# Where a first norm's squares are made, and which bank holds a sixth row: a change to the opening stage of a two-layer recurrent decoder step

## The chip, the cores and the metric

The kernel runs on one core of one Trainium2 chip. The metric is the device time of one execution in microseconds (us), smaller being better. The time before the change is 1043.81 us, the median of 3 runs (1042.59 to 1045.02).

In the profile the engines are PE (TensorE, matrix products), DVE (VectorE), ACT (ScalarE), POOL (GpSimd) and SP (SyncE, which here issues most of the DMAs). Each engine works through its own instructions in the order in which the program lists them.

## The reference, cut to what matters

The reference is one step of a decoder with two layers: a gated linear recurrence with a short convolution (RG-LRU) and then a layer with a matrix state (HGRN2). There are 1024 prompt tokens and 32 sample tokens, 1056 columns in all. Everything is float32. The change touches the first lines of the first layer:

```python
def _rmsnorm(x, gain):
    y = x * lax.rsqrt(jnp.mean(x * x, axis=-1, keepdims=True) + EPS)
    return y * gain

def _lru_layer(x, g_norm, w_in, ...):
    xn = _rmsnorm(x, g_norm)
    u = xn @ w_in                       # 1024 -> 2 * 1536
    xb, gate = u[..., :W_LRU], u[..., W_LRU:]
    xc, new_buf = _causal_conv(xb, conv_w, conv_b, buf)
    h, h_last = _rg_lru(xc, w_r, b_r, w_i, b_i, lam, h0)
    y = h * silu(gate)
    return x + y @ w_out, h_last, new_buf
```

The scale `rsqrt(mean(x*x))` is one number for each token. It can be applied before the product or, because the product is linear, to its result.

## The kernel before, in words

**Tiles.** The activations lie transposed: 8 tiles (k = 0 to 7) of 128 features by 1056 tokens, cut into 3 chunks of 352 tokens. A float32 product is made from three faster matmuls: every operand is split into a high part (a cast, on ACT) and a low part (the difference, on DVE or POOL), and `mm3` (lines 288 to 290) adds high by high, high by low and low by high. One output row of 128 features for one chunk is 8 steps of k, so 24 matmuls, collected in one PSUM bank. There are eight banks: four of the tag `mm`, which take the rows in turn, and four of the tag `hg`, used in turn for norms and for the small products of the recurrence.

**The opening stage** (`start`, `begin`, `products`, lines 947 to 1018) makes six output rows (three gate rows, then three convolution rows) for each chunk.
- *Chunk 0* goes unnormed. Its x is multiplied by the gain and split as it lands (lines 958, 959), and its scale is applied when a row leaves its bank: line 610 for a gate row, line 563 for a convolution row. The scale comes from `squares` (line 481: the squares at line 488 on POOL or line 490 on ACT, their sum over k by the DVE additions of line 492) and from `norm` (line 496): a sum over features by PE (line 325), mean plus EPS by DVE (line 505), the power -0.5 by POOL (line 530), a diagonal by DVE (lines 531, 534), its spreading over 128 partitions by PE (line 536) and a copy to SBUF by ACT (line 990). That copy is what lines 610 and 563 multiply with.
- *Chunks 1 and 2* are normed ahead of their products. `token_norm` loads their tokens a second time, tokens by features (t0, t1, t2), squares and sums them on ACT (line 523), and spreads the scale in the same way (lines 524, 530, 531, 534, 536). `scaled_parts` then multiplies x by gain and scale (line 541, DVE), casts it (line 542, ACT) and subtracts (line 373, DVE, for two of eight tiles POOL).

Before the change four of the eight squares (k = 1, 3, 5, 7, the tuple `MU`) are made by POOL and four by ACT, through two buffers in turn. The weights of a row come in halves: `w0a`, `w0b` to `w5a`, `w5b`. Each half is loaded (line 358), cast on ACT (line 432) and subtracted (line 373), on DVE for rows 0, 1, 2 and 4 and on POOL for rows 3 and 5. Row 4 of chunk 0 has a `hg` bank (`ASIDE`); row 5 takes an `mm` bank again, the one that row 0 used.

**Order.** `Flow` (line 61) collects every operation with its engine, an estimated duration and its data dependences. `run` plans forward, then backward (`back`), which gives every operation its latest start as a key; smaller keys go first among the operations that are ready. It does so eight times, then tries 3000 random changes to the keys of the first 60 us (`search`), and issues all engines' instructions in the planned order. A second `Flow` does the same for the second layer, starting from the times at which the first leaves its buffers. Operations with a `chain` keep the order in which they were added: `FIRST_S` and `FIRST_Q` are the first loads on the ACT and SP queues, `FIRST` the order in which ACT and DVE prepare what has landed, `NEXT` the further loads on the SP queue. In them `x0` is a tile of chunk 0, `X0` one of chunk 1, `P` and `hc` small parameters.

Of the kernel before, what the change touches and what calls it, by code (L numbers as in the profile page):

```python
# [24 lines left out]
NW, NXO, NRAW = 4, 3, 3  # L25
# [8 lines left out]
SPOTS, SPOTS0, SPOTS1 = (-1, -1, 0, 2), (2, 5, -1, -1), (1, 5, 9, 13, 17, 20)  # L34
K2 = 8 - K1
MEAN = 4.0
ASIDE = (4,)
ASIDE_W = ()
FIRST_S = "x0 g0 w0b x4"
FIRST_Q = "w0a x1 x2 x3 x5 x6 x7 w1a w1b"  # L40
FIRST = "w0a x0 x1 x2 x3 w0b x4 x5 x6 x7 w1a w1b"
NEXT = "w2a w2b t0 w3a w3b t1 w4a w4b -w4a t2 X0 X1 X2 X3 w5a w5b X4 X5 X6 X7 P hc"
RM, SM = 3, 6
OUT = ((0, 512), (512, 288), (800, 256))

# [15 lines left out]
class Flow:  # L61
# [9 lines left out]
    def __init__(self, until=None, side=1.2, busy=None, given=None):  # L71


        self.until = until
        self.busy = {e: (busy or {}).get(e, 0.0) for e in self.ENGINES}
        self.exact = busy is not None
        self.side = side
        self.ops = []
        self.writer = {}
        self.readers = {}  # L80
        self.main = None
        self.chain = {}
        self.soft = set()
        self.given = given or {}
        self.born = []
        self.lead = {}

    def add(self, eng, us, emit, r=(), w=(), prio=5, kb=0, main=False, both=False, line=None):

# [140 lines left out]
    def run(self, tries=0, first=0.0):  # L230
        self.after = [[] for _ in self.ops]
        for i, o in enumerate(self.ops):
            for d in o[3]:
                self.after[d].append(i)
        best = got = self.plan([o[4] for o in self.ops])
        for _ in range(self.TURNS):
            got = self.plan(self.back(got[2], got[4]))
            self.ends.append(got[0])
            best = min(best, got, key=lambda g: g[0])
        if tries:  # L240
            best = self.search(best, tries, first)
        self.log = [(i, self.ops[i][0], best[1][i], best[2][i]) for i in best[3]]
        for i in best[3]:
            self.ops[i][2]()
# [12 lines left out]
def tile_trunk(ctx: ExitStack, tc: tile.TileContext, xT, xN, prm, hc, w0, wg, wo0, w1, wo1, s_in,  # L257
               yT, h_out, c_out, sp_out, ss_out):
    nc = tc.nc
    V, S, G, T, Q = nc.vector, nc.scalar, nc.gpsimd, nc.tensor, nc.sync  # L260
# [13 lines left out]
    P = const.tile([128, NPRM], F32, name="prm_sb")  # L274
# [8 lines left out]
    def chunk(c):  # L283
        return slice(c * CH, (c + 1) * CH)
# [34 lines left out]
    def spans(n):  # L319
        return [(a, min(128, n - a)) for a in range(0, n, 128)]  # L320
# [23 lines left out]
    with ExitStack() as l0:  # L344
        pl = l0.enter_context(tc.tile_pool(name="l0", bufs=1, reuse_waits="tile"))
        fl = Flow("PE")

        def fixed(name, shape, dt=F32, pool=None):
            return (pool or pl).tile(shape, dt, tag=name, name=name)

        def ring(name, n, cols=CH, dt=F32):
            return cycle([(pl.tile([128, cols], dt, tag=f"{name}{i}", name=f"{name}_{i}"), (name, i)) for i in range(n)])
# [8 lines left out]
        def act(n, emit, r, w, prio=5, more=0.0, chain=None):  # L361
            fl.add("ACT", (0.09 + 0.00088 * n if fl.exact else 0.25 + 0.0007 * n) + more, emit, r, w, prio, line=chain)
# [5 lines left out]
        def pool(n, emit, r, w, prio=5):  # L368
            fl.add("POOL", 0.13 + 0.0022 * n if fl.exact else 0.1 + 0.00245 * n, emit, r, w, prio)
# [16 lines left out]
        t0 = fixed("t0", [128, 3, NB])  # L386
# [4 lines left out]
        xbs = ring("xb", 3, 384)  # L391
        ks = [(KR[:, chunk(i)], ("k", i)) for i in range(KB)]
        ts, xrs = cycle(ks[:3]), cycle(ks[3:])
        xos = ring("xo", NXO)
# [88 lines left out]
        def squares(k, x, xk, acc, eng=None, own=None, mult=False, chains=(None, None)):  # L483

            a, ak = acc
            sq, sk = next(own or ts) if k else acc
            if mult:
                pool(CH, lambda: G.tensor_tensor(sq[:, :CH], x, x, op=ALU.mult), (xk,), (sk,), 2)
            else:
                act(CH, lambda: S.activation(sq[:, :CH], x, AF.Square), (xk,), (sk,), 2, chain=chains[0])  # L490
            if k and eng is V:
                dve(CH, lambda: V.tensor_tensor(a[:, :CH], a[:, :CH], sq, op=ALU.add), (sk, ak), (ak,), 2, chain=chains[1])
            elif k:
                pool(CH, lambda: G.tensor_tensor(a[:, :CH], a[:, :CH], sq, op=ALU.add), (sk, ak), (ak,), 2)
# [14 lines left out]
        def token(c, i, prio, chain=None):  # L509

            (t, tk), (a, u) = tspots[c][i], spans(CH)[i]
            q = slice(c * CH + a, c * CH + a + u)
            dma(t[:u, :D], xN[q], (), tk, prio, 4 * u, chain=chain)
# [415 lines left out]
        free = [(R2[s][:, i, j], ("R", s, i, j)) for s in range(2) for i in range(2) for j in range(3)]  # L929
        raw = (halves[1][:8], [slots[i] for i in (4, 7, 5, 8)] + [halves[1][8], free[8], free[0], free[1]], free[2:8] + free[9:11])  # L930
        g0s = [g0[:, k:k + 1] for k in range(KD)]
        sqs, bcs = cycle([next(xos) for _ in range(NXO - 1)]), next(xos)
        acc, MU = next(xbs), (1, 3, 5, 7)
        VI = (0, 1, 2, 4)
        tspots = ((), ((rows[0], [slots[i][1] for i in range(3)]), (KR[:, :D], [k for _, k in ks[:3]]),
                       (R[:, 3], [("R", 1, 1, j) for j in range(3)])),
# [10 lines left out]
        def start():  # L947

            steps = {"P": [lambda q, c: dma(P, prm, (), (("P",),), 0, 74, q, c)],
                     "g0": [lambda q, c: dma(g0, prm[:, PRM["g0"][0]:PRM["g0"][1]], (), (("g0",),), 0, 4, q, c)]}  # L950
            for k, (x, xk) in enumerate(raw[0]):
                a, b = xh[k][:, chunk(0)], xl[k][:, chunk(0)]

                def load(q, c, k=k, x=x, xk=xk):
                    dma(x, xT[k][:, chunk(0)], (), (xk,), 0, 180, q, c)

                def parts(chains, k=k, x=x, xk=xk, a=a, b=b):
                    act(CH, lambda: S.activation(a, x, AF.Copy, scale=g0s[k]), (xk, ("g0",)), (("xh", k, 0),), 1, chain=chains[0])
                    dve(CH, lambda: V.scalar_tensor_tensor(b, x, g0s[k], a.bitcast(F32), op0=ALU.mult, op1=ALU.subtract),
                        (xk, ("g0",), ("xh", k, 0)), (("xl", k, 0),), 1, True, chains[1])  # L960

                steps[f"x{k}"] = load, parts
            for i in range(6):
                ahead = []
                row(i, ahead)
                for j, (load, split) in zip("ab", ahead):
                    steps[f"w{i}{j}"] = lambda q, c, load=load: load(q=q, chain=c), split
            steps.update({f"t{i}": [lambda q, ch, i=i: token(1, i, 1.0, ch)] for i in range(3)})
            steps.update({f"X{k}": [lambda q, ch, k=k: fetch(1, (k,))] for k in range(KD)})
            steps["hc"] = [lambda q, ch: dma(hct, hc, (), (("hct",),), 2, 196, q, ch)]  # L970
            for q, names in ((S, FIRST_S), (Q, FIRST_Q)):
                for n in names.split():
                    steps[n][0](q, str(q))
            done = FIRST.split()
            for n in done:
                steps[n][1](("ACT0", "DVE0"), *([G] if n in ASIDE_W else []))
            for n in NEXT.split():
                if n[0] == "-":
                    steps[n[1:]][1]()
                    done.append(n[1:])  # L980
                else:
                    steps[n][0](Q, SPQ)
            for i in range(6):
                for j in "ab":
                    if f"w{i}{j}" not in done:
                        steps[f"w{i}{j}"][1]()
            for k, (x, xk) in enumerate(raw[0]):
                squares(k, x, xk, acc, V, sqs, k in MU, ("ACT0", "DVE0"))
            bc, bk = norm(acc, next(xrs))
            act(CH, lambda: S.copy(bcs[0], bc), (bk,), (bcs[1],), 0)  # L990

        def fetch(c, ks=range(KD)):

            for k in ks:
                x, xk = raw[c][k]
                dma(x, xT[k][:, chunk(c)], (), (xk,), (0, 1.4, 1.9)[c], chain=SPQ)
# [7 lines left out]
        def products(c):  # L1004
            for i in (2, 0, 1, 3, 4, 5) if c else range(6):
                items[i][1](c, *product(ws[i], xcols(c), 1, later[i], next(hg) if not c and i in ASIDE else None), *([] if c else [bcs]))

# [46 lines left out]
    with ExitStack() as l1:  # L1054
        p1 = l1.enter_context(tc.tile_pool(name="l1", bufs=1, reuse_waits="tile"))
        last = {e: max(t[3] for t in fl.log if t[1] == e) for e in Flow.ENGINES}
        fl = Flow(side=0.4, busy={e: max(0.0, t - last["PE"]) for e, t in last.items()}, given=fl.times(last["PE"]))
# [651 lines left out]
        for k in range(H):  # L1709
            if k < 4:  # L1710
                olds = [("x", 1, k, x) for x in range(2)] + [("T", 1, i, k, x) for i in range(2) for x in range(2)]
            else:
                n, i = ((2, 0), (3, 0), (4, 0), (4, 1))[k - 4]
# [36 lines left out]
        x2 = [Gs, R[:, 3], R[:, 2], R[:, 1], Bs, B2, VT, Gc]  # L1750
# [5 lines left out]
        for n, (m, c) in enumerate([(m, c) for c in range(NCH) for m in range(2)] + [(m, c) for m in range(2, KD) for c in range(NCH)]):  # L1756
# [9 lines left out]
            x, xk = x2[m][:, chunk(c)], ykeys(Y2 + m, c * CH, CH)  # L1766
# [13 lines left out]
        for m in range(KD):  # L1780
# [4 lines left out]
            raw, rk = next(raws)  # L1785
# [12 lines left out]
        accs, sqs, dgs, sb = cycle(spare[:2]), cycle(spare[2:5]), cycle(spare[5:7]), spare[7]  # L1798
# [47 lines left out]
        for a, n in OUT:  # L1846
# [3 lines left out]
            acc, ak = next(accs)  # L1850
            for m in range(KD):
# [13 lines left out]
                x, xk = x2[m][:, q], ykeys(Y2 + m, a, n)  # L1865
# [88 lines left out]
```

## Time and profile before

| | |
|---|---|
| median of 3 runs | 1043.81 us |
| the profiled execution's own time | 1044.79 us |
| its span, first to last instruction | 1043.0 us |
| mean granted TensorE clock | 0.995 |
| PE busy | 1030.1 us, 99% of the span |
| DVE, ACT, POOL busy | 793.5, 590.4, 502.1 us |

The span leaves 1.8 us of the execution's time outside. A timeline row gives the start, the duration, the engine, the line and operation, the tile written and the tiles read, and in brackets how long the engine sat idle before it and what ended that. "x2" is two instructions merged in one row. `PEclk` is the clock that the throttle granted, as a part of full speed. A row of the windows view gives for each engine the busy time in that stretch and, behind an x, the number of instructions that started there.

### The profile page before, as it was taken

The page shows a single profiled execution, that of the slowest core. Times are in us where ns is not written, and L with a number is a line of the kernel's source. Part 1 is how long each engine was busy: PE and PEld are TensorE (multiplying, and loading weights), DVE is VectorE, ACT ScalarE, POOL GpSimd, SP SyncE. Part 2 cuts the span into 40 slices and gives each one's busy share as a digit, 9 for nine tenths or more (in the row PEclk, how much of TensorE's full clock was granted, in tenths as well). Part 3 has the DMA queues.
Part 4 walks back from the last instruction along what each step waited for, and adds up shares of the span by engine and source line. Part 5 has one row for each costly group of instructions (what it writes and reads, how often), then busy time and mean ns, then how long its engine had stood idle before and what let it go on. Part 6 is the DMA issues. An engine that isn't in the chain of part 4 may idle for free.

```text
span 1043.0 us, 25410 instructions
## 1 busy us (share of the span) xinstructions
PE 1030.1 (99%) x9794; PEld 1001.2 (96%) x9794; DVE 793.5 (76%) x1539; ACT 590.4 (57%) x1345; POOL 502.1 (48%) x587
## 2 busy tenths in 40 slices
PE   9899999999999999999999999999999999999997
PEld 9899999999999999999999999999999999989986
DVE  6899997888897599345498987877969696984436
ACT  6678656877775775334445464647464555752324
POOL 3325343444534355643527565554645555641544
PEclk9999999999999999999999999999999999999998
DMA  9511112123661586544655151423233242666204
GB/s 295 182 29 50 51 53 75 55 63 98 212 200 52 160 275 182 155 135 154 215 162 154 59 170 45 149 72 123 86 106 122 87 139 85 220 189 210 87 1 167
DMA packets 92809, 133.55 MB, mean 128 GB/s; under 512 B 11728, under 2 KB 70096, under 8 KB 92688
## 3 DMA queue, kind: packets, MB, share of 16 engines
q1 hardware_dynamic: 82896, 115.50, 35.3%
q10 hardware_dynamic: 9792, 16.43, 4.9%
q8 instruction: 77, 1.26, 0.5%
q14 instruction: 44, 0.36, 0.1%
HBM read 88.81 MB, written 38.20 MB: 122 GB/s over the span
## 4 chain that ended last, share of the span: by engine, by line
PE 95%; DMA 2%; issue 1%; DVE 1%; POOL 0%; SPq 0%; ACTq 0%; ACT 0%; POOLq 0%; DVEq 0%
PE mm L288 27%; PE mm L290 26%; PE mm L289 26%; PE hg L1185 2%; PE hg L650 1%; PE hg L1399 1%; PE hg L288 1%; PE hg L1401 1%; PE hg L289 1%; PE hg L290 1%; PE hg L1347 1%; DMA k<-in_xN_dram 1%; PE mm L1347 1%; PE hg L1443 1%; DMA wraw<-in_w_dram 1%
## 5 line engine op out<-in xcount | busy, mean ns | idle before, releaser
L288 PE MATMUL mm<-xh,whi 128*128 128x352 f32 (+1 forms) x1127 | 351.4, 312 | 0.0
L290 PE MATMUL mm<-xh,wlo 128*128 128x352 f32 (+1 forms) x1127 | 347.7, 308 | 0.0
L289 PE MATMUL mm<-xl,whi 128*128 128x352 f32 (+1 forms) x1127 | 347.3, 308 | 0.0
L373 POOL TENSOR_TENSOR wlo<-wraw,whi 128x256 fp32r<-128x256 f32 (+3 forms) x180 | 193.8, 1095 | 199.8 <-ACT whi L432 102.3
L289 PEld LDWEIGHTS mm<-xl,whi 128*128 128x128 f32 x1127 | 212.3, 188 | 1.5
L288 PEld LDWEIGHTS mm<-xh,whi 128*128 128x128 f32 x1127 | 211.7, 188 | 1.7
L290 PEld LDWEIGHTS mm<-xh,wlo 128*128 128x128 f32 x1127 | 212.0, 188 | 0.0
L288 PE MATMUL mm<-t,whi 128*128 128x264 f32 (+1 forms) x330 | 96.8, 293 | 1.3 <-DVE sg L1641 1.3
L582 DVE SCALAR_TENSOR_TENSOR k<-xb,prm_sb,k 128x352 f32<-128x352 f32 (+2 forms) x144 | 87.8, 619 | 12.9 <-ACT k L579 9.3
L290 PE MATMUL mm<-t,wlo 128*128 128x264 f32 (+1 forms) x330 | 94.4, 286 | 0.0
L289 PE MATMUL mm<-t,whi 128*128 128x264 f32 (+1 forms) x330 | 94.3, 286 | 0.0
L373 POOL TENSOR_TENSOR wlo<-R,whi 128x256 fp32r<-128x256 f32 x78 | 67.2, 887 | 44.5 <-ACT whi L1564 32.6
L1641 DVE TENSOR_TENSOR k<-mm,k 128x264 f32<-128x264 f32 x118 | 49.7, 425 | 22.9 <-PE mm L290 22.3
L665 POOL TENSOR_TENSOR k<-X 128x352 f32<-128x352 f32 x36 | 42.9, 1200 | 48.8 <-DVE R L666 39.0
L288 PEld LDWEIGHTS mm<-t,whi 128*128 128x128 f32 x330 | 62.0, 188 | 2.6 <-DVE sg L1641 1.8
L290 PEld LDWEIGHTS mm<-t,wlo 128*128 128x128 f32 x330 | 62.1, 188 | 0.0
L289 PEld LDWEIGHTS mm<-t,whi 128*128 128x128 f32 x330 | 62.1, 188 | 0.0
L432 ACT CAST whi<-wraw 128x512 fp32r<-128x512 f32 (+2 forms) x79 | 43.9, 572 | 25.7 <-PE mm L289 9.7
L288 PE MATMUL mm<-yh,whi 128*128 128x352 f32 x153 | 50.0, 327 | 0.0
L289 PE MATMUL mm<-yl,whi 128*128 128x352 f32 x153 | 49.4, 323 | 0.0
L290 PE MATMUL mm<-yh,wlo 128*128 128x352 f32 x153 | 49.4, 323 | 0.0
L1564 ACT CAST whi<-R 128x512 fp32r<-128x512 f32 x39 | 24.1, 617 | 35.1 <-PE mm L289 33.2
(479 smaller groups left out, 2521.5 us busy)
## 6 DMA issues: line engine op xcount, KB each, us to landing
wraw<-in_w_dram SPq DMA_DIRECT2D x54, 256.0 KB, 3.2
wraw<-in_w_dram ACTq DMA_DIRECT2D x34, 256.0 KB, 3.5
wraw<-in_wo_dram SPq DMA_DIRECT2D x34, 192.0 KB, 2.5
R<-in_w_dram ACTq DMA_DIRECT2D x19, 256.0 KB, 2.8
si<-in_s_in_dram SPq DMA_DIRECT2D x8, 512.0 KB, 5.6
vt<-sg SPq DMA_DIRECT2D x8, 512.0 KB, 3.3
sg<-vt SPq DMA_DIRECT2D x32, 128.0 KB, 3.0
kt<-kt SPq DMA_DIRECT2D x8, 512.0 KB, 2.6
```

The lines of the kernel that those rows point to most:

```text
L288: T.matmul(out, wh, xh, start=first, stop=False, skip_group_check=more)
L289: T.matmul(out, wh, xl, start=False, stop=False, skip_group_check=more)
L290: T.matmul(out, wl, xh, start=False, stop=last, skip_group_check=more)
L373: emit = lambda: e.tensor_tensor(b, x, a.bitcast(F32), op=ALU.subtract)
L432: act(m, lambda: S.copy(hi[:, :m], raw[:, :m]), rk, (hk,), prio, chain=chains[0])
L582: dve(u, lambda src=src, dst=dst, sh=sh, k=k: V.scalar_tensor_tensor(dst, sh(src, k), pc("cw", 12 * k + m), dst, op0=ALU.mult, op1=ALU.add ...
L650: fl.add("PE", 0.62, lambda ps=ps, i=i, c=c: T.matmul(ps[:96, :CH], gs[:, i, :], ST[:96, chunk(c)], start=True, stop=True), (("gs",), *((" ...
L665: pool(CH, lambda x=x, a=a, b=b: G.tensor_tensor(x, a.bitcast(F32), b.bitcast(F32), op=ALU.add), (ak, bk), (xk,), 3)
L1185: T.matmul(ps[32 * j:32 * j + 32, n * w:n * w + w], B[:, o:o + 32], q(slice(o, o + 32)), start=True, stop=True, tile_position=(0, 32 * j))
L1347: T.matmul(ps[:, n * 128:(n + 1) * 128], kt[:, 4 * i + n, :], vt[:, 4 * i + n], start=True, stop=True)
L1564: act(512, lambda: S.copy(hi, raw), (rk,), (hk,), 2)
L1641: dve(QT, lambda: V.tensor_tensor(o[0], z[0], u[0], op=ALU.add), (z[1], u[1]), (o[1],), 0)
```

## The change

- All eight squares of chunk 0 are made on ACT; `MU` is gone. They go through seven buffers instead of two: six places in the tile `R` that lie free at that time, and one `xo` buffer.
- The squares and their additions, `s0` to `s7`, get a place in the fixed order of ACT and DVE: four behind `w2b`, four behind `w3b`. The order of `FIRST` now runs through the halves `w2a` to `w3b`.
- The squares, the additions and the whole norm of chunk 0 with its copy get their keys lowered by 8 us (`PUSH`) in each of the planning turns, so that they go ahead of other ready work.
- On the SP queue the loads `X4` and `X5` of chunk 1 go ahead of `w5a` and `w5b` instead of behind them. The other loads keep their order.
- Row 5 of chunk 0 gets a `hg` bank, as row 4 has. The rows behind it take the banks of both tags one place further on in turn.

```diff
-ASIDE = (4,)
-ASIDE_W = ()
+ASIDE = (4, 5)
+PUSH = 8.0
 FIRST_S = "x0 g0 w0b x4"
-FIRST_Q = "w0a x1 x2 x3 x5 x6 x7 w1a w1b"
-FIRST = "w0a x0 x1 x2 x3 w0b x4 x5 x6 x7 w1a w1b"
-NEXT = "w2a w2b t0 w3a w3b t1 w4a w4b -w4a t2 X0 X1 X2 X3 w5a w5b X4 X5 X6 X7 P hc"
+FIRST_Q = "w0a x1 x2 x3 x5 x6 x7 w1a w1b w2a w2b t0 w3a w3b"
+FIRST = "w0a x0 x1 x2 x3 w0b x4 x5 x6 x7 w1a w1b w2a w2b s0 s1 s2 s3 w3a w3b s4 s5 s6 s7"
+NEXT = "t1 w4a w4b -w4a t2 X0 X1 X2 X3 X4 X5 w5a w5b X6 X7 P hc"
...
+        self.push = {}
...
-            got = self.plan(self.back(got[2], got[4]))
+            got = self.plan([k - self.push.get(i, 0.0) for i, k in enumerate(self.back(got[2], got[4]))])
...
-        sqs, bcs = cycle([next(xos) for _ in range(NXO - 1)]), next(xos)
-        acc, MU = next(xbs), (1, 3, 5, 7)
+        bcs, acc = next(xos), next(xbs)
+        sqs = cycle(free[2:8] + [next(xos)])
...
+            for k, (x, xk) in enumerate(raw[0]):
+                steps[f"s{k}"] = None, lambda chains, k=k, x=x, xk=xk: squares(k, x, xk, acc, V, sqs, False, chains)
...
-                steps[n][1](("ACT0", "DVE0"), *([G] if n in ASIDE_W else []))
+                a = len(fl.ops)
+                steps[n][1](("ACT0", "DVE0"))
+                if n[0] == "s":
+                    fl.push.update(dict.fromkeys(range(a, len(fl.ops)), PUSH))
...
-            for k, (x, xk) in enumerate(raw[0]):
-                squares(k, x, xk, acc, V, sqs, k in MU, ("ACT0", "DVE0"))
+            n = len(fl.ops)
             bc, bk = norm(acc, next(xrs))
             act(CH, lambda: S.copy(bcs[0], bc), (bk,), (bcs[1],), 0)
+            fl.push.update(dict.fromkeys(range(n, len(fl.ops)), PUSH))
```

## The prediction

> **What bounds the kernel now.** I read the page's first part, then busy time by stretches, then PE's timeline where PE has gaps, then the chain of waits backwards from the largest gap.
>
> ```profile
> PE 1030.1 (99%) x9794; PEld 1001.2 (96%) x9794; DVE 793.5 (76%) x1539; ACT 590.4 (57%) x1345; POOL 502.1 (48%) x587
> ```
> ```profile
> 24.20:38.22 14.02, 10.96 (x54) 9.95 (x53) 11.45 (x28) 8.94 (x19) 7.68 (x10) 0.88 0.97 338
> 38.22:61.60 23.38, 23.38 (x146) 23.17 (x145) 20.09 (x55) 13.97 (x37) 5.69 (x11) 1.00 0.11 30
> ...
> 400.00:1000.00 600.00, 598.47 (x7155) 580.16 (x7154) 436.34 (x902) 292.71 (x753) 311.39 (x363) 1.00 0.42 132
> 1000.00:1043.00 43.00, 35.70 (x237) 32.37 (x236) 22.29 (x48) 17.26 (x41) 21.32 (x23) 0.93 0.29 102
> ```
> ```profile
> 29.90:33.32 3.42, 1.36 (x8) 1.06 (x7) 3.42 (x8) 3.33 (x8) 0.98 (x1) 0.99 1.04 345
> 33.32:36.74 3.42, 3.42 (x13) 3.42 (x13) 3.42 (x9) 2.90 (x7) 2.33 (x4) 0.51 0.99 380
> ```
>
> PE is the bound. It is idle for 13 us of the span: 7.3 us at the end, 1.5 us between 400 and 1000, and 3.06 us between 24.20 and 38.22, which is rows 4 and 5 of chunk 0. Only the last lies where the change is. The stretch loses more than its idle time: it holds 54 matmuls, and the next one runs 146 in 23.38 us, 0.160 each. At that pace 54 take 8.6 us, plus 0.5 us for the two slow spreading products among them, so 9.1 us; it took 14.02. **About 4.9 us can be won here.** The last fence says where the part that isn't idle went: just behind the emptiest stretch the granted clock is 0.51 for 3.42 us, a loss of 0.49 x 3.42 = 1.7 us. 3.06 + 1.7 = 4.8 agrees.
>
> ```profile
> 22.61 0.69 PE L325 MATMUL hg<-ones,xb 128*128 128x1 f32 x6
> ...
> 25.17 0.75 PE L536 MATMUL hg<-k,ones 128*128 128x352 f32 x2
> ...
> 28.84 0.86 PE L536 MATMUL hg<-k,ones 128*128 128x352 f32 x2 [0.99 <-DVE k L534]
> ...
> 32.72 0.43 PE L288 MATMUL mm<-xh,yh 128*128 128x352 f32 x1 [2.06 <-DVE sg L610]
> ...
> 38.22 0.32 PE L288 MATMUL mm<-xh,X 128*128 128x352 f32 x1
> ```
> ```profile
> 26.14 0.87 POOL nr L530
> ...
> 32.23 0.44 DVE sg L610
> ...
> 57.21 0.59 PE hg L536 x2
> ```
> ```profile
> 20.21 2.26 DVE L492 TENSOR_TENSOR xb<-xb,xo 128x352 f32<-128x352 f32 x2
> ...
> 24.12 0.43 DVE L531 TENSOR_TENSOR k<-ident,nr 128x256 f32<-128x256 f32 x1 [0.97 <-POOL nr L530]
> ...
> 24.77 0.15 DVE L505 TENSOR_SCALAR nr<-hg 128x2 f32<-128x2 f32 x1
> ...
> 27.04 1.56 DVE L531 TENSOR_TENSOR k<-ident,nr 128x256 f32<-128x256 f32 x1 [2.06 <-POOL xb L556]
> ...
> 29.31 0.58 DVE L541 SCALAR_TENSOR_TENSOR sg<-sg,g,hg 128x352 f32<-128x352 f32 x1 [0.40 <-issue]
> 29.80 0.57 DVE L541 SCALAR_TENSOR_TENSOR R<-R,g,hg 128x352 f32<-128x352 f32 x1
> ...
> 30.79 0.52 DVE L373 TENSOR_TENSOR xl<-sg,xh 128x352 fp32r<-128x352 f32 x1
> ```
>
> There are two gaps. At 28.84 PE has, next in its order, the spreading of chunk 0's scale, and waits 0.99 us for the diagonal. At 32.72 row 5 has waited 2.06 us for line 610, which empties row 0's bank and needs that same scale. Read backwards it is one chain: the last addition of squares ends at 22.47, PE sums at 22.61, line 505 comes at 24.77, the power at 26.14, the diagonal at 27.04, the spreading at 28.84, the copy at 31.30 (row below), and the bank is free at 32.67. DVE sits idle from 24.98 to 27.04 inside this chain, and starts on chunk 1 (line 541) only at 29.31, though chunk 1's own scale was spread at 25.17.
>
> **The change part by part.**
>
> *Row 5 in a gate bank.* It removes row 5's wait for line 610. Its new bank is the one in which PE sums the squares of chunk 0, free once line 505 has read it: 24.98 in this trace. PE would reach row 5 at 24.20 + 24 x 0.160 + 2 x 0.59 (the spreadings, by the last row of the chain) = 29.2. No wait is left, and the margin is over 4 us. Worth 2.06 us, and the 1.7 us of low clock if the gap caused it. Next to need row 0's bank is row 2 of chunk 1, at 29.2 + 3.9 = 33.1.
>
> *Squares on ACT.*
>
> ```profile
> L492 DVE TENSOR_TENSOR xb<-xb,xo x7: 510/525/1631, 12.1 to 21.9; 128x352 f32<-128x352 f32 x7
> L488 POOL TENSOR_TENSOR xo<-sg x4: 772/774/1161, 5.0 to 18.9; 128x352 f32<-128x352 f32 x4
> L490 ACT ACTIVATE xo<-sg x3: 481/496/496, 11.6 to 19.5; 128x352 f32<-128x352 f32 x3
> ```
> ```profile
> 13.18 0.62 ACT L432 CAST X<-a 128x512 fp32r<-128x512 f32 x1 [0.61 <-DMA a<-in_w_dram]
> 14.78 1.06 ACT L523 ACTIVATE sg<-sg 128x1024 f32<-128x1024 f32 x1 [0.97 <-DMA sg<-in_xN_dram]
> ...
> 16.74 0.60 ACT L432 CAST yh<-ST 128x512 fp32r<-128x512 f32 x1
> ...
> 24.19 1.30 ACT L432 CAST yh<-wraw 128x512 fp32r<-128x512 f32 x2 [1.25 <-DMA wraw<-in_w_dram]
> ...
> 31.30 0.44 ACT L990 COPY xo<-hg 128x352 f32<-128x352 f32 x1
> ```
> ```profile
> 16.51 1.30 POOL L373 TENSOR_TENSOR yl<-a,yh 128x512 fp32r<-128x512 f32 x1 [0.35 <-ACT yh L432]
> ...
> 19.64 1.82 POOL L373 TENSOR_TENSOR yl<-ST,yh 128x512 fp32r<-128x512 f32 x1
> ...
> 24.89 1.30 POOL L373 TENSOR_TENSOR yl<-wraw,yh 128x512 fp32r<-128x512 f32 x1 [0.80 <-ACT yh L432]
> ...
> 38.10 1.31 POOL L373 TENSOR_TENSOR xl<-R,xh 128x352 fp32r<-128x352 f32 x1
> ```
> ```profile
> 19.73 0.32 PE L288 MATMUL mm<-xh,yh 128*128 128x352 f32 x1
> ```
>
> POOL loses 4 x 0.77 = 3.1 us, ACT gains 4 x 0.5 = 2.0 us. ACT has the room: the rows show it waiting for data 0.61, 0.97 and 1.25 us. But the order is fixed now. w2b's cast ends at 13.80; four squares take 2.0 us and t0's squares (1.06) may come between, so w3a and w3b are cast by 16.9 + 1.2 = 18.1, against 17.34 now. They go on to POOL: 17.5 + 1.30 = 18.8 for the first half and 18.8 + 1.82 = 20.6 for the second. Row 3 wants them at 19.73 and, twelve matmuls later, 21.65. Margins of about 1 us: cost nothing. If that cover is gone, each us of lateness is a us of PE.
>
> The second four squares follow w3b. At the earliest (w3b cast at its present time, 17.34) they end at 19.3 and the last addition at about 19.9; at the latest, with t1's squares and row 4's two casts ahead, at 22, no later than the 22.47 of now. I take 20.5: the buffers no longer force square, addition, square in turn, and the lowered keys put them ahead of the casts.
>
> *The norm first.* From the last addition the steps are 0.69 for PE's sum, 2 x 0.15 for line 505 (which comes twice), 0.87 for the power, 0.43 and 0.24 for the diagonal (28.60, where line 531 ends, to 28.84), 0.59 and 0.44: 3.6 us, and with some 0.1 us at each of six handovers, an estimate, about 4.2 where nothing stands ahead. Now it is 9.3 us (22.47 to 31.74), because the token norm is ahead on DVE and the split of w5a on POOL, and the diagonal shares its time with the split of w5b (1.56 us). From 20.5 the copy ends near 25 to 26. Line 610 empties row 0 near 26, needed at 33.1. Even if every obstacle stayed, 22 + 9.3 = 31.3, and 0.9 on is still in time. PE's own wait at the spreading (0.99 us) depends on how well the plan's guess meets the chip, since PE waits in order: between 0 and 0.99 for each of its two norm products, more only if the additions slip. I take 0.5 us in all, as two of the three large obstacles (the buffers, w5's splits) are out of the way.
>
> *X4, X5 ahead of w5a, w5b.*
>
> ```profile
> 17.64 0.33 SPq L358 DMA_DIRECT2D wraw<-in_w_dram  x1
> 20.32 0.33 SPq L358 DMA_DIRECT2D wraw<-in_w_dram  x1
> 20.69 0.42 SPq L358 DMA_DIRECT2D sg<-in_xT_dram  x1
> 21.78 0.33 SPq L358 DMA_DIRECT2D R<-in_xT_dram  x1
> ```
> ```profile
> R<-in_xT_dram SPq DMA_DIRECT2D x11, 176.0 KB, 3.9
> ```
>
> The loads move 338 GB/s at 97% of the DMA engines, so two tiles of 176 KB take about 1.0 us of it. w5a comes 1 us later: cast at 25.2, split on POOL by 27.2, w5b by 28.5; row 5 wants them at 29.2 and 31.1. Covered by 2 us. w5b waits for a buffer until 20.32 either way, and X6 and X7 stay near 22.
>
> *What is late next: chunk 1.* PE wants its first low part at 33.1 and the eighth at 36.5. DVE can start when the scale is there, 25.17 + 0.75 = 25.9. Eight multiplications at 0.49 (29.31 to 29.80) and six subtractions at 0.52 are 7.0 us; emptying six rows adds 6 x 0.44 = 2.6: done at 35.5 if DVE does nothing else, and four of those six needn't come first. POOL's two subtractions of 1.31 are beside it. It fits with 1.0 us to spare, but DVE has also gate and convolution work, so I charge 0.4 us.
>
> Sum: -4.8 + 0.5 + 0.4 = -3.9, rounded to **-4.0 us**. The profiled execution took 1044.79 us, so 1040.8; it lies 0.98 us over the median of the three runs, and from the median I forecast **1039.8 us**.
>
> [...] The row says that 2.06 us of idle time within a 3.42 us stretch was followed by 3.42 us at a clock of 0.51. [...]
>
> **The rivals.**
>
> *Chunk 1 becomes the wait.* Today its eighth low part is ready at 38.10 + 1.31 = 39.4. If DVE starts on it no earlier than now, PE, there at 33.1, does its last step at 39.4 instead of 36.5 and loses 2.9 us: a gain of 2.0, or of 0.5 if a low clock follows again. For it: DVE is busy in all of 29.90 to 36.74, and the norm's work moves in front of it. Against: 2.06 us idle at 27.04. 1041.8 to 1043.3.
>
> [...]
>
> *Slower: PE held at the norm's sum.* With keys lowered, the plan puts PE's sum of squares early among the rows, counting each addition at its free 0.52 us. On the chip one took 1.63 beside POOL work. PE then stands still until the last addition. A hold of w us costs w, and above some 2 us the 1.7 of low clock as well: at w = 3.1 the gain is gone, beyond it the kernel is slower; w = 5 gives 4.0 - 6.7, so 1046.5. It needs three or four additions delayed by 1.1 us. Only the two splits of row 3 are left on POOL there, so two delays can be, four hardly.
>
> *It doesn't do what it says.* A search follows the planning and may move the norm back. Then only the bank helps: this is the first rival with the 0.99 us gap kept, a gain of about 1.
>
> **How the numbers follow.** About 0.2%, 2.1 us, is what a measurement of this kernel can tell from no change. Forecast (a gain of 3 to 5 us): 0.60. Low clock stays: 0.08, mostly still faster. Chunk 1 late, or the norm moved back: 0.25, a third of it above 2.1 us. PE held: 0.07. Faster 0.60 + 0.05 + 0.08 = 0.73; slower 0.06; same 0.21. For the range: below, the whole 4.9 us and 1.3 us for a kinder plan of the end (1.5 us idle before 1000 and 7.3 behind it can shift either way, as the plan is drawn anew), so 1037.6; above, the late chunk 1 without most of its gain, 1043.2.
>
> **What would show it.** Right: PE busy without a gap from 8 to 60 us; row 2 of chunk 1 starting at 33 to 34 instead of 38.22; PEclk 1.00 there; the copy of line 990 before 28; line 541 first seen near 26; the last 43 us as now. Wrong: a wait of PE at line 325 or 536 (held), at line 288 for DVE's line 373 (chunk 1), or at 19.73 for POOL's splits of row 3; or the opening won and as much lost behind 400 us.

## The result, and the profile after

The kernel after takes 1040.99 us (median of 17 runs, 1038.15 to 1042.43), the one before 1043.81 us (17 runs, 1042.44 to 1045.21). The ratio is 0.9973, with a 95% interval of 0.9965 to 0.998: 2.8 us faster, between 2.1 and 3.7. The forecast was 1039.8 us, a gain of 4.0 us, with a range from 1037.6 to 1043.2 us. Two single runs far from all others, one of the kernel before at 5706 us and one of a version below at 1169 us, are left out of the ratios and the counts of runs below.

In the profile of after every line number behind the edits is one to six higher (288 is 289, 373 is 374, 536 is 537, 541 is 542, 610 is 611, 990 is 995). First the page's first part and the busy time by stretches:

```profile
PE 1027.8 (99%) x9794; PEld 998.9 (96%) x9794; DVE 791.1 (76%) x1539; ACT 592.1 (57%) x1349; POOL 504.3 (49%) x583
```
```profile
24.20:38.22 14.02, 14.02 (x86) 13.60 (x85) 12.97 (x29) 8.14 (x24) 5.75 (x6) 1.00 0.88 285
38.22:61.60 23.38, 22.30 (x137) 21.62 (x135) 21.87 (x55) 16.23 (x38) 8.69 (x12) 1.00 0.17 53
...
400.00:1000.00 600.00, 598.57 (x7150) 579.39 (x7149) 433.00 (x897) 292.13 (x752) 311.81 (x362) 1.00 0.41 131
1000.00:1039.00 39.00, 31.75 (x220) 29.18 (x219) 20.90 (x46) 16.26 (x39) 18.75 (x21) 0.92 0.32 112
```

The stretch from 24.20 to 38.22 is full now: 86 matmuls where there were 54, at a clock of 1.00. The next stretch, full before, has lost 1.08 us. The end is as it was. PE's timeline says where the waits are (the rows with an idle time in brackets, and those that answer to the rows of before):

```profile
21.29 0.78 PE L326 MATMUL hg<-ones,xb 128*128 128x1 f32 x6 [0.35 <-DVE xb L493]
25.84 0.75 PE L537 MATMUL hg<-k,ones 128*128 128x352 f32 x2
28.36 0.75 PE L537 MATMUL hg<-k,ones 128*128 128x352 f32 x2
...
33.30 0.32 PE L289 MATMUL mm<-xh,X 128*128 128x352 f32 x1
...
61.49 0.43 PE L290 MATMUL mm<-xl,X 128*128 128x352 f32 x1 [1.08 <-POOL xl L374]
```

Row 2 of chunk 1 begins at 33.30 instead of 38.22. The two waits of before (0.99 and 2.06 us) are gone. Two others have come: 0.35 us at the sum of squares, and 1.08 us in chunk 2, for a low part that POOL makes. DVE, ACT and POOL at the norm, from their timelines:

```profile
20.71 0.53 DVE L493 TENSOR_TENSOR xb<-xb,xo 128x352 f32<-128x352 f32 x1
22.96 0.17 DVE L525 TENSOR_SCALAR nr<-nr 128x3 f32<-128x3 f32 x1 [1.73 <-ACT R L524]
23.04 0.21 DVE L506 TENSOR_SCALAR nr<-hg 128x2 f32<-128x2 f32 x2
...
25.80 1.30 DVE L535 TENSOR_SCALAR k<-ident,nr 128x96 f32<-128x96 f32 x1
...
27.22 1.07 DVE L542 SCALAR_TENSOR_TENSOR sg<-sg,g,hg 128x352 f32<-128x352 f32 x2
...
31.10 0.94 DVE L611 TENSOR_TENSOR sg<-mm,xo 128x352 f32<-128x352 f32 x2
```
```profile
21.78 1.06 ACT L524 ACTIVATE R<-R 96x1024 f32<-96x1024 f32 x1 [2.09 <-DMA R<-in_xN_dram]
...
22.84 1.13 ACT L433 CAST yh<-wraw 128x512 fp32r<-128x512 f32 x2
...
30.13 0.45 ACT L995 COPY xo<-hg 128x352 f32<-128x352 f32 x1
```
```profile
24.09 0.86 POOL L531 TENSOR_TENSOR nr<-nr,mhalf 128x3 f32<-128x3 f32 x1
25.74 1.29 POOL L374 TENSOR_TENSOR yl<-wraw,yh 128x512 fp32r<-128x512 f32 x1 [0.79 <-ACT yh L433]
28.91 1.47 POOL L374 TENSOR_TENSOR yl<-wraw,yh 128x512 fp32r<-128x512 f32 x1 [1.88 <-ACT yh L433]
```

The last addition ends at 21.24 (22.47 before), but the copy of the scale starts only 1.2 us sooner than it did: 30.13 against 31.30. What was won at the squares (1.23 us) reaches the copy, but the way between the two is no shorter: 9.3 us from the end of the last addition to the end of the copy, as before. On it DVE waits until 22.96 for the token norm of chunk 1, whose last load ACT could not take up before 21.78, and reads the sum of squares only behind that. The power comes behind that of the token norm, the last piece of the diagonal takes 1.30 us beside the split of w5a, and the copy stands behind chunk 1's casts on ACT. It is in time all the same, since PE needs row 0's bank at 33.30 and line 611 has emptied it at about 31.6.

### The profile page after: what moved, and what is told of

The parts are those of the page before. It is cut to its first block, busy times and chain, and to the rows that moved or that the text cites. A ratio compares the mean times of both kernels' runs of the same rounds, so it can differ in the third digit from the quotient of the medians.

```text
span 1039.0 us, 25402 instructions
## 1 busy us (share of the span) xinstructions
PE 1027.8 (99%) x9794; PEld 998.9 (96%) x9794; DVE 791.1 (76%) x1539; ACT 592.1 (57%) x1349; POOL 504.3 (49%) x583
## 4 chain that ended last, share of the span: by engine, by line
PE 92%; DMA 2%; DVE 2%; issue 1%; SPq 1%; POOL 1%; ACT 1%; POOLq 0%; ACTq 0%; DVEq 0%
PE mm L289 26%; PE mm L291 25%; PE mm L290 25%; PE hg L1191 2%; PE hg L651 1%; PE hg L1405 1%; PE hg L1407 1%; PE hg L289 1%; PE hg L290 1%; PE hg L291 1%; DMA R<-in_xN_dram 1%; SPq L359 1%; PE hg L1353 1%; PE mm L1353 1%; PE hg L1449 1%
## 5 line engine op out<-in xcount | busy, mean ns | idle before, releaser
L374 POOL TENSOR_TENSOR wlo<-wraw,whi 128x256 fp32r<-128x256 f32 (+3 forms) x180 | 198.4, 1121 | 186.5 <-ACT whi L433 98.4
L647 ACT ACTIVATE R<-hg,smalls 128x352 f32<-128x352 f32 x72 | 38.0, 553 | 12.8 <-DVE R L687 7.3
```

Source lines behind the costliest of these rows:

```text
L374: emit = lambda: e.tensor_tensor(b, x, a.bitcast(F32), op=ALU.subtract)
L647: act(CH, lambda ps=ps, R=R, i=i, j=j, hb=hb, m=m: S.activation(R[:, i, j], ps[:, :CH], AF.Tanh, bias=hb[:, m:m + 1], scale=0.5), (pk, ("s ...
```

## The experiments

The theory to test (A): the gain comes from the date at which line 610 empties row 0, held against the date at which PE wants that bank; the bank for row 5 moves the second by one row, the early norm the first. Rivals: one of the two parts is the whole of it; the plan that happened to be drawn is; the low clock has nothing to do with the gap. Each kernel below was timed beside the kernel before on the same chip.

**The bank alone.** The kernel before with

```
-ASIDE = (4,)
+ASIDE = (4, 5)
```

> The kernel before with one edit: row 5 of chunk 0 gets a gate bank, the squares and the loads stay. Theory A (the bank takes away the 2.06 us wait at row 5, but chunk 1 is then the bound, since DVE begins line 541 no earlier than about 29): PE reaches chunk 1 near 34 us, waits there 1 to 2.5 us for the low parts of line 373, and the kernel gains 1 to 2 us on before. Rival B (the bank is the whole of the change, the early norm adds nothing): a gain of 2.5 to 3 us, as the full change has, and no wait before chunk 1.

Measured: 0.9984 (0.9976 to 0.9993), a gain of 1.7 us. PE's wait, the DVE operation that ends it, and the copy of the scale:

```profile
35.14 0.43 PE L288 MATMUL mm<-xh,X 128*128 128x352 f32 x1 [1.60 <-DVE sg L610]
```
```profile
34.57 0.51 DVE L610 TENSOR_TENSOR sg<-mm,xo 128x352 f32<-128x352 f32 x1
```
```profile
32.17 0.45 ACT L990 COPY xo<-hg 128x352 f32<-128x352 f32 x1
```

The size is A's, the mechanism isn't quite: PE waits not for a low part of chunk 1 but for the same line 610 as before, one row further on. The bank moves the wait; it doesn't take away what makes it. Nor is the norm alone what makes it here: the copy ends at 32.62, and DVE comes to line 610 only 1.95 us later, behind its work on chunk 1 (0.41 us in before). So the date of line 610 depends on DVE's order too.

**Everything but the bank.** The kernel after with

```
-ASIDE = (4, 5)
+ASIDE = (4,)
```

> The kernel after with row 5 of chunk 0 back on the bank that row 0 used; squares on ACT, order and lowered keys stay. Theory A (both parts are needed): the norm comes earlier than in before, but its copy is not ready before 29 to 30, so row 5, due at about 29, waits 0.5 to 1.5 us for the line that empties row 0, too little for a low clock; a gain of 1.5 to 2.5 us on before. Rival B (the bank is the whole of it): row 5 waits some 2 us as before and the gain is under 1 us. Rival C (the early norm is the whole of it): no wait, and a gain of 2.5 to 3 us.

Measured: 0.9975 (0.9965 to 0.9984), 2.6 us.

```profile
30.80 0.43 PE L289 MATMUL mm<-xh,yh 128*128 128x352 f32 x1 [0.74 <-DVE sg L611]
```
```profile
30.23 0.94 DVE L611 TENSOR_TENSOR sg<-mm,xo 128x352 f32<-128x352 f32 x2
```

Row 5 waits 0.74 us, as A expected, in an execution with a mean clock of 0.996, but the gain is the one of rival C (2.5 to 3 us), just above A's (1.5 to 2.5). There is no other wait before 70 us: the 1.08 us at chunk 2 are absent. PE's first product of chunk 2 comes at 60.42 in this profile and at 58.01 in after's, while POOL's low parts end at about 61.4 in both. So with the bank 0.74 us go at row 5 and 1.08 us come at chunk 2; beside the rest of the change the bank has no gain that can be measured.

**Without the lowered keys.** The kernel after with

```
-PUSH = 8.0
+PUSH = 0.0
```

> The kernel after with PUSH 0, so that the squares and the norm get no lowered keys; squares on ACT, seven buffers, fixed order, loads and bank stay. Theory A (with the bank there are microseconds of slack at the norm): the same as after within 0.8 us, a gain of 2 to 3.5 us on before. Rival (the keys bring the norm forward): the sum of squares and the spreading come 2 us later or more, chunk 1 waits, and the gain is 1.5 us or less.

Measured: 0.9994 (0.9985 to 1.0003), no gain that can be told from nothing. A's number fell, the rival's held.

```profile
36.15 0.43 PE L289 MATMUL mm<-xh,X 128*128 128x352 f32 x1 [3.09 <-DVE sg L611]
```
```profile
35.58 0.95 DVE L611 TENSOR_TENSOR sg<-mm,xo 128x352 f32<-128x352 f32 x2
```
```profile
34.61 0.45 ACT L995 COPY xo<-hg 128x352 f32<-128x352 f32 x1
```

The copy comes at 34.61, later than in before, and the bank's extra row is eaten up. The slack that I had counted on at the norm isn't a property of the work: without the keys the plan uses it up.

**The keys and the bank, squares as before.** The kernel before with `ASIDE = (4, 5)`, the lines of `push` in `Flow`, and the squares where they were:

```
+            n = len(fl.ops)
             for k, (x, xk) in enumerate(raw[0]):
                 squares(k, x, xk, acc, V, sqs, k in MU, ("ACT0", "DVE0"))
...
+            fl.push.update(dict.fromkeys(range(n, len(fl.ops)), PUSH))
```

> The kernel before with the bank for row 5 and with the keys of the squares and the norm lowered by 8 us; the squares stay on POOL and ACT with two buffers and without a new place in the order, the loads stay. Theory E (the lowered keys bring the copy of the scale forward, the squares on ACT add little): copy at 31 or earlier, no wait before chunk 1 above 0.5 us, a gain of 2 to 3 us on before. Rival F (the squares through two buffers keep the sum back however the keys stand): the sum of squares at 23 or later, the copy at 31.5 or later, a wait of 0.8 us or more at row 2 of chunk 1, a gain under 2 us.

Measured: 0.9984 (0.9976 to 0.9993), 1.7 us. Copy at 32.36, and:

```profile
33.91 0.43 PE L290 MATMUL mm<-xh,X 128*128 128x352 f32 x1 [0.31 <-DVE sg L612]
```

Rival F's dates and gain, but a smaller wait than it said. The wait is 1.29 us shorter than with the bank alone and the gain is the same; with intervals of 0.9 us to either side that neither shows a use of those 1.29 us nor rules one out. The squares on ACT, with their place in the order, bring the copy forward (32.36 to 30.13, the loads' order being another difference), and the keys do it too (34.61 to 30.13); neither alone has it in time without a wait.

**The old order of the loads.** The kernel after with

```
-NEXT = "t1 w4a w4b -w4a t2 X0 X1 X2 X3 X4 X5 w5a w5b X6 X7 P hc"
+NEXT = "t1 w4a w4b -w4a t2 X0 X1 X2 X3 w5a w5b X4 X5 X6 X7 P hc"
```

> The kernel after with the old order of the loads: w5a and w5b ahead of X4 and X5. Theory A' (the loads' order is not what the gain comes from): the same as after within 0.8 us, no wait of PE for chunk 1 above 0.5 us. Rival (X4 and X5 behind w5b, which waits for its buffer until about 24, come too late for chunk 1): PE waits 1 us or more before 38 and the gain on before is under 2 us.

Measured: 0.9975 (0.9964 to 0.9987), as after.

```profile
33.99 0.43 PE L289 MATMUL mm<-xh,X 128*128 128x352 f32 x1 [0.63 <-DVE sg L611]
38.73 0.43 PE L290 MATMUL mm<-xl,X 128*128 128x352 f32 x1 [0.96 <-POOL xl L374]
```

The time is as A' said, the waits aren't: it allowed no wait above 0.5 us at chunk 1. They sit there now, and chunk 2 has none: 1.59 us in sum against 1.43 in after. The order of the loads moves the waits and not the time.

**Another plan.** The kernel after with `rng = Random(2)` for `Random(1)`.

> The kernel after with another seed of the random search, nothing else: what part of the gain is the one plan that was drawn. Theory A' (the gain comes from when the copy of chunk 0's scale is made and from the bank): copy before 31.5, no wait of PE between 23 and 40 above 0.5 us, a gain of 2 to 3.5 us on before; the place and size of the small waits (0.35 at the sum, 1.08 at chunk 2) may change. Rival (the plan that was drawn makes it): a wait of over 1 us at another place before 40 and a gain under 1.5 us.

Measured: 0.9977 (0.9968 to 0.9986), copy at 30.51, no wait of PE from 8 to 70 us above 0.2. It isn't the one plan. This plan has no waits in the opening and still isn't measurably faster than after. One reason that a single profile can't settle this: its first product starts at 8.68 us, 0.99 later than the 7.69 of after's profile, and both spans are 1039.0.

**Chunk 2's low parts on DVE.** The kernel after with

```
-            scaled_parts(c, k, x, xk, bc, bk, g0s[k], ("g0",), G if k % 4 == 3 else V)
+            scaled_parts(c, k, x, xk, bc, bk, g0s[k], ("g0",), G if k % 4 == 3 and c < 2 else V)
```

The low parts from 52 to 64 us in after, by engine (durations least, median, most in ns):

```profile
L374 DVE TENSOR_TENSOR xl<-R,xh x6: 512/514/1246, 56.2 to 60.6; 128x352 fp32r<-128x352 f32 x6
L374 POOL TENSOR_TENSOR xl<-R,xh x2: 1212/1827/2442, 57.8 to 60.2; 128x352 fp32r<-128x352 f32 x2
```

> The kernel after with the two low parts of chunk 2 that POOL makes (k = 3 and 7) given to DVE; chunks 0 and 1 stay. Theory D (the 1.08 us wait of PE at 61.5 in after is for POOL's second low part, which shares its time with DVE's work and takes 1.8 us instead of 1.0 to 1.3): the wait goes or falls under 0.3 us, and the kernel gains 0.7 to 1.1 us on after, 3.3 to 4.2 on before. Rival (DVE, busy in all of 55 to 60, is what chunk 2 waits for): the wait stays or grows and there is no gain on after.

Measured: 0.997 (0.9959 to 0.998), 3.1 us; PE has no wait at all from 8 us to past 900. Once more, beside after on one chip:

> The kernel after with chunk 2's two POOL low parts given to DVE, a second time, on the chip of the kernel above. Theory D (the wait at chunk 2 was POOL's): no wait of PE at chunk 2, 0.5 to 1.3 us faster than after on the same chip, 3 to 4 us faster than before. Rival (its first measurement, 3.1 us faster than before, is within the scatter of after's): no difference from after beyond 0.3 us.

> The kernel after, unchanged, on the chip of the kernel below, to compare the two directly: a gain of 2 to 3 us on before, PE waiting some 1.1 us at chunk 2 (for a low part of POOL) and some 0.3 us at the sum of squares, no run at a clock of 0.995 or less.

Measured: this version 0.9969 (0.9958 to 0.998), 1040.09 us; after 0.9977 (0.9968 to 0.9986), 1040.78 us, with the wait of after's profile there again:

```profile
61.27 0.43 PE L290 MATMUL mm<-xl,X 128*128 128x352 f32 x1 [0.82 <-POOL xl L374]
```

That the wait was POOL's is shown: it is there in both profiles of after and in neither of this version. That the version is faster than after isn't: 0.7 us lie within the intervals. It beats before in both measurements.

**The low clock.** First the kernel before once more, unchanged.

> The kernel before, unchanged, to see whether its low clock is there in each execution. [...] Rival (the gap always halves the clock): 3.4 us at a clock of 0.5 behind the gap again, about 1.6 us lost.

Measured: 1.0002 (0.9991 to 1.0012). The same two waits at the same places, from PE's timeline, and the clock in three stretches of 3.4 us, about the length of the low one in the first profile:

```profile
28.57 0.86 PE L536 MATMUL hg<-k,ones 128*128 128x352 f32 x2 [0.90 <-DVE k L534]
...
32.46 0.43 PE L288 MATMUL mm<-xh,yh 128*128 128x352 f32 x1 [2.07 <-DVE sg L610]
```
```profile
28.45:31.86 3.41, 1.82 (x8) 1.32 (x8) 2.94 (x8) 2.19 (x5) 0.00 (x0) 1.00 1.05 351
31.86:35.27 3.41, 2.81 (x17) 2.81 (x18) 3.41 (x9) 3.21 (x8) 2.67 (x4) 1.00 1.00 285
35.27:38.69 3.42, 3.42 (x24) 3.42 (x23) 3.42 (x9) 2.38 (x5) 2.15 (x3) 1.00 1.00 367
```

No low clock follows: 1.00 in all three, where the first profile has 0.51 from 33.32 to 36.74 behind a gap of 2.06 us. So the expectation's rival fell: the gap doesn't halve the clock each time. The kernel without lowered keys has the longest gap of all, 3.09 us, and its profiled execution keeps its clock as well:

```profile
31.57:34.98 3.41, 1.49 (x8) 1.02 (x6) 3.41 (x8) 2.91 (x8) 1.97 (x2) 1.00 0.91 282
34.98:38.40 3.42, 2.25 (x14) 2.25 (x15) 3.12 (x8) 2.46 (x7) 2.24 (x4) 1.00 0.96 350
```

The runs say how often it happens: of the 68 runs of before made up to then 24 have a mean granted clock of 0.995 or less, with a median of 1044.6 us; the other 44 have 1042.9. The share is 0.35, and the difference is the 1.7 us of the half-rate stretch. Of 28 runs of after none has such a clock. (The mean also holds the end of the run, with 0.93 from 1000 us on in the first profile of before, so the figure alone is no proof for a kernel with another end: two of seven and two of eleven runs of two versions without a wait in the opening show 0.995 as well.) How long a gap must be, and why the same gap is followed by a low clock in one execution and not in another, isn't settled by this: 4 of 12 runs without the keys, 3 of 11 with the bank alone and 1 of 11 with keys and bank are at 0.995 or less too, five of these eight at 0.994 or 0.993, although the profiles of the last two show gaps of 1.60 and 0.31 us only. To see whether the gap is the cause, it was filled:

```
+        def spin():
+            for _ in range(4):
+                T.matmul(sumbank[0][:, :128], ones, ones, start=True, stop=True)
...
                     for k in ks:
                         mm3(ps[:, :CH], w(k)[:2], *xs[k][:2], k == 0, k == n - 1)
+                    if tail and k == n - 1:
+                        tail()
```

with `tail=spin` for row 4 of chunk 0 alone, and `sumbank` the bank of the norm's sums.

> The kernel before with one addition: behind row 4 PE makes four small matmuls of ones, 0.9 us, into the bank of the norm's sums, whose content has been read by then, so that the 2.06 us for which PE waits at row 5 are no longer all idle. The wait itself, the plan and every other instruction stay. Of 68 runs of before, 24 had a mean granted clock of 0.995 or less, with a median of 1044.6 us, the other 44 of 1042.9. [...] Rival (the low clock comes and goes for a reason outside this gap): a third of the runs at 0.995 or less again, and the time unchanged.

Measured: 0.9998 (0.9989 to 1.0007), and of 11 runs none at 0.995 or less.

```profile
30.68 1.05 PE L502 MATMUL hg<-ones 128*128 128x128 f32 x8
32.91 0.43 PE L288 MATMUL mm<-xh,yh 128*128 128x352 f32 x1 [1.17 <-DVE sg L619]
```

Row 5 starts as late as ever, and the clock stays up, at 1.00 from 29.21 to 36.04. The 23 runs of before beside it had 5 at 0.995 or less, at 1044.4 us in the median, the other 18 at 1043.1; this kernel is at 1043.2. So the gap is very probably what halved the clock in those runs of before. Were it not, 11 runs without a low clock would come about once in 70 times at the rate of all 91 runs of before (29 of them low), and once in 15 at the rate of the 23. The profile adds nothing to this, since the second one of before kept its clock with the gap unfilled. The average gain of about 0.5 us that this should give lies inside the interval and isn't shown.

## Why the prediction was right, point by point

*The direction and both waits* were right. The wait at row 5 and the one at the spreading are gone, 86 matmuls ran where there were 54, row 2 of chunk 1 starts at 33.30 (said: 33.1), the clock there is 1.00, and the squares' place in the order cost row 3 nothing.

*Which part does it* was wrong. The prediction put the whole 2.06 us wait, and the clock behind it, down to the bank. The bank alone gains 1.7 us, with the same line waited for one row on; everything but the bank gains 2.6. What is needed is the earlier norm, and for it the lowered keys: without them the gain is gone, bank and all.

*The size.* The step that failed is the term **"the 1.7 us of low clock if the gap caused it"**, taken into the sum in full. The gap very probably caused it, but only in the profiled execution and in about a third of the runs: 24 / 68 x 1.7 = 0.6 us on average, 1.1 less than was put in. The forecast of 4.0 less 1.1 is 2.9; measured 2.8. That this comes so near is partly luck: the waits that are left took 1.43 us instead of 0.9, and some 0.6 us of gain have no known source (below). Between the two profiled executions, of which the one of before has the half rate, the difference is 4.0 us: 1044.79 and 1040.79. Of that, 1.6 us are waits, 1.7 the clock, and 0.39 only a first product that happened to start sooner. The hint stood in the table: the profiled execution lay 0.98 us over the median of the three runs, and I carried that over as an offset instead of asking what in it was not in the others.

*A low clock that stays though the gap goes*, with a chance of 0.08, becomes improbable by the filled gap: of the 11 runs with it none is at 0.995 or less. Without the clock's 1.7 us the forecast would have been 1041.5 us, nearer to the measured 1040.99 than 1039.8 is, but for another reason: the 1.7 us count for a third only. Nor was the gap enough by itself: in the first profile of before 2.06 us were followed by 3.42 us at 0.51, in the second 2.07 us by a clock of 1.00. What decides between the two was not shown.

*What is late next* stopped too early. I charged chunk 1 with 0.4 us and it cost none, and the norm products with 0.5 us where the sum took 0.35. Chunk 2 wasn't looked at, and cost 1.08 us (0.82 in a second profile). PE reaches it 5.4 us sooner (58.01 instead of 63.42), while DVE and POOL make its low parts together from 57 to 61.

*The norm's date* was wrong by 4 to 5 us: copy said for 25 to 26, before 28 at the latest; measured 30.13. Chunk 1's multiplications (line 541, said near 26) began at 27.22. My free-way sum of 4.2 us held for none of the kernels; the shortest way, in the version without the bank, took 8.75 us. The last addition of squares was roughly right: 21.24, said 20.5. And "even if every obstacle stayed, still in time" was wrong outright: without the keys the copy comes at 34.61 and PE waits 3.09 us. Row 2 of chunk 1 found its bank free all the same, because the keys hold the date at 30 and the bank allows 33.

*The loads.* w5b was to wait for its buffer until 20.32 either way; it is issued at 24.19, from SP's timeline, because the casts of w4 slid to 22.84:

```profile
20.14 0.33 SPq L359 DMA_DIRECT2D wraw<-in_w_dram  x1
...
24.19 0.33 SPq L359 DMA_DIRECT2D wraw<-in_w_dram  x1
```

Its split ends at 30.4 (28.91 + 1.47) instead of 28.5. Row 5 begins its second half twelve matmuls before 33.30, at 31.4: the cover of over 2 us was down to 1.0.

*Rivals.* Chunk 1 as the next wait is what the bank alone shows, at its price (a gain of 1.7, said 0.5 to 2.0) though for a bank and not for a low part. PE held at the norm's sum is there, at 0.35 us. Its break-even was worked out wrongly: a hold of 3.1 us uses up 4.8 us of gain, the forecast's 4.0 are used up at 2.3, if the low clock follows, which it did not behind 2.07 us in the second profile of before and 3.09 us without the keys; and the sum before it, -3.9, was rounded to -4.0. What is left of the 2.8 us beside the waits (3.05 - 1.43 = 1.6) and the clock (0.6), some 0.6 us, has no known source; the plan behind 60 us is also a new one.

## What to carry to other kernels

Take a wait's end as a date and its user's need as another, and say which of the two an edit moves: a further bank moved only the need, by one row, and the same line was waited for again there. When a stage is sped up, check every later stage that now starts earlier, not the next one alone. And before a stretch of low clock goes into a sum, count in how many runs it is there; a profiled execution well over the median is the sign to do so.

## What the runs showed of the hardware

In the first profile of before PE's gap of 2.06 us, which ended at 32.72, was followed by a granted clock of 0.51 from 33.32 to 36.74, 3.42 us. A gap of 2.07 us in the second profile was followed by a clock of 1.00, and so was one of 3.09 us in the kernel without lowered keys. The start differs too. In the first profile of before, PE's timeline of the warm-up, cut at 5.94 and at 5.96 us:

```profile
1.05 5.16 PE L812 MATMUL hg<-ones 128*128 128x128 f32 x23 [1.05 <-DVE nr L500]
```
```profile
5.69 2.53 PE L812 MATMUL hg<-ones 128*128 128x128 f32 x20
```

Up to there 23 take 5.16 us, some 0.22 each; behind it 20 take 2.53 us, little more than half of that each. The granted clock of the windows view reads 1.00 on both sides, so what quickens them was not shown. In the first profile of after the change comes 0.8 us earlier, at about 5.15, and the first product starts at 7.69 instead of 8.08, in the one of the other plan at 8.68, with the same 21 warm-up products in each. The other thing is how long a small DVE step can be beside a POOL split: line 535's 96 columns took 1.30 us at 25.80, next to the split at 25.74, and 0.25 us at 24.48, with no split beside it. Of such pairs only the low parts of chunk 2 were taken apart in an experiment.
